# Gated linear attention: the two heads' half-height products issued in turn into two banks

## The chip, the cores and the metric

One core of one Trainium2 chip runs the whole program. The metric is the time of one execution on the device in microseconds (us); where several runs are compared, it is their median. The five engines of a core are TensorE (PE in the rows, its weight loads PEld), VectorE (DVE), ScalarE (ACT), GpSimd (POOL) and SyncE (SP).

## The reference

The program is one inference step of a two-layer decoder for 512 prompt tokens and 8 sample tokens at a model width of 1024. Layer 0 mixes tokens with differential attention and with gated linear attention (GLA), layer 1 with an mLSTM; each mixer stands between two half-step feed-forward blocks. The change touches only the GLA of the prompt: 4 heads with 64 key and 128 value features.

```python
b = jnp.cumsum(g, axis=2)                       # log decay, per key feature
decay = jnp.exp(jnp.where(causal, b_t - b_s, -inf))
a_intra = einsum('bnthd,bntshd,bnshd->bnhts', q, decay, k)
o_intra = einsum('bnhts,bnshv->bnthv', a_intra, v)
...
o_inter = einsum('bnthd,bnhdv->bnthv', q * exp(b), s_prev)
return o_intra + o_inter, s_fin
```

## The kernel before, in words

All tensors lie with features on the 128 partitions and tokens along the free dimension. Stage `even` is layer 0's mixer. Inside it `gla_pair(p, more)` runs twice, for p = 0 and p = 1. A pair is two heads: head i of the pair has its 64 key features on partitions 64i to 64i+63 of `bq[p]` and `bk[p]`.

A pair works on four chunks of 128 tokens (j = 0 to 3). Within a chunk the decay between two tokens is split by levels: at level lv the chunk falls into blocks of `64 >> lv` tokens, and the decay to the middle between two neighbouring blocks is folded into a scaled copy `gkq` of keys and queries (`level`, two DVE products per level). For each of the 8 masks (one for the diagonal, 7 levels) and each head, the inner function `masked` (lines 895 to 905) takes one PSUM bank, called `glv`, lets PE form four 128 by 128 products, one per chunk, with a contraction over the 64 partitions of that head (line 899), and lets DVE copy the masked entries into the head's matrix `A[i]` (`copy_predicated`, line 901). The products are in f32; the profile counts two PE records for each f32 product. Then `masked` calls `tick` and `aside`. At the end of a pair (lines 966 to 975), for each head in turn, a bank `go` collects per chunk `bv` times `A[i]` (contraction over 128, line 971) and, from the second chunk on, the state `S` times the scaled queries `qt` (contraction over the head's 64 partitions, line 974), and ACT evicts the bank to `ob`.

What else stands around these products on the in-order PE: `tick(us)` adds to an account, and whenever it holds more than 1.65 it issues a step of the sample tokens' attention (`sample_steps`). In this part a step is 8 products `so` of 128 by 32 columns (line 776, four column groups of the array), and needs one `vtile` of two pages (2 x 256 KB) that SP's queue loads from the cache; four such buffers rotate. `aside` advances generators that share the time: `gla_sample` (products `gsu` with a contraction over 8 partitions, line 1011, and `gso`), the head norms (`hs`, `hst`, `bc`) and splits. `decays` forms the decays of a level (`gdc`, line 914). `more` yields the projections of the output gate, `pj` (lines 100 to 102, full-height products); all four of its yields are used up in pair 0. After pair 1 stands the output projection, `y`, on the same three lines.

The banks for `glv`, `go`, `gdc`, `hs`, `bc` and the like come from one pool, `pmm`, of four PSUM banks that rotate (`bank`, line 615). Two banks are kept for dense products and two for the long sums of the sample attention. A scheduler places the instructions on each engine's queue; each engine then takes its own queue in order.

Of the kernel before, what the change touches and what calls it, by code (L numbers as in the profile page):

```python
# [15 lines left out]
P = 128  # L16
D = 1024
KT = 8
SEQ = 512
# [15 lines left out]
STEP, ORATE, GLAX = 1.65, 3.3, 1.7  # L35
# [20 lines left out]
class Net:  # L56
# [829 lines left out]
    def gla_pair(self, p, more):  # L886

        nc, gl = self.nc, self.gl
        bv = self.bv[p]
        q, k = self.bq[p], self.bk[p]  # L890
        A = [gl.tile([P, 512], F32, tag=f"A{i}", name="A") for i in range(2)]
        for a in A:
            nc.gpsimd.memset(a, 0.0)

        def masked(i, lhs, rhs, lv):
            r = slice(64 * i, 64 * i + 64)
            ps = self.bank("glv")
            for j in range(4):
                nc.tensor.matmul(ps[:, j * P:j * P + P], lhsT=lhs[r, j * P:j * P + P], rhs=rhs[r, j * P:j * P + P],  # L899
                                 start=True, stop=True)  # L900
            nc.vector.copy_predicated(A[i].rearrange("p (j t) -> p j t", j=4),
                                      self.gmask[:, lv, None, :].to_broadcast([P, 4, P]),
                                      ps.rearrange("p (j t) -> p j t", j=4))
            self.tick(0.9 * GLAX)
            self.aside()

        def decays(lv, n):

            e = gl.tile([P, 2, 4, P], F32, tag="ge", name="ge", bufs=2)[:, :n]
            for j in range(4):  # L910
                ps = self.bank("gdc")
                r = self.lvl[:, lv * P:(lv + n) * P]
                for i, s in enumerate((self.gh, self.gl_)):
                    nc.tensor.matmul(ps[:, :n * P], lhsT=s[:, j, p * P:p * P + P], rhs=r, start=(i == 0), stop=(i == 1))
                nc.scalar.activation(e[:, :, j, :], ps[:, :n * P].rearrange("p (l t) -> p l t", l=n), AF.Exp)
                self.tick(0.12 * n * GLAX)
            return e.rearrange("p l j t -> p l (j t)")

        if p == 0:
            next(more, None)  # L920
        ec = decays(7, 2)
        es = [decays(0, 2)]
        eb, er = ec[:, 0, :], ec[:, 1, :]
        qt = gl.tile([P, 512], F32, tag="gqt", name="gqt")
        nc.vector.tensor_tensor(out=qt, in0=q[:, :SEQ], in1=eb, op=ALU.mult)
        nc.vector.tensor_tensor(out=er, in0=k[:, :SEQ], in1=er, op=ALU.mult)
        next(more, None)
        kn = gl.tile([P, 4, P], F32, tag="gkn", name="gkn")
        self.natural(kn, None, er)
        S = []  # L930
        for j in range(4):
            ps = self.bank("gu")
            for i in range(2):
                nc.tensor.matmul(ps[64 * i:64 * i + 64, :P], lhsT=kn[:, j, 64 * i:64 * i + 64],
                                 rhs=bv[:, j, i, :], start=True, stop=True)
            s = gl.tile([P, P], F32, tag=f"S{j}", name="S")
            if j == 0:
                self.evict(s, ps[:, :P])
            else:
                nc.vector.scalar_tensor_tensor(s, S[-1], eb[:, j * P + P - 1:j * P + P], ps[:, :P], ALU.mult, ALU.add)  # L940
            S.append(s)
        nc.scalar.dma_start(out=self.t["o_gp"][p], in_=S[3])
        def level(lv):
            w = 64 >> lv
            ev = es[lv // 2][:, lv % 2, :].rearrange("p (n s w) -> p n s w", s=2, w=w)
            kv = k[:, :SEQ].rearrange("p (n s w) -> p n s w", s=2, w=w)
            qv = q[:, :SEQ].rearrange("p (n s w) -> p n s w", s=2, w=w)
            kq = gl.tile([P, 512], F32, tag="gkq", name="gkq", bufs=2)
            kqv = kq.rearrange("p (n s w) -> p n s w", s=2, w=w)
            nc.vector.tensor_tensor(out=kqv[:, :, 0, :], in0=kv[:, :, 0, :], in1=ev[:, :, 0, :], op=ALU.mult)  # L950
            nc.vector.tensor_tensor(out=kqv[:, :, 1, :], in0=qv[:, :, 1, :], in1=ev[:, :, 1, :], op=ALU.mult)
            return kq
        kq = level(0)
        for i in range(2):
            masked(i, k, q, 7)
        for lv in range(7):
            if lv in (0, 2):
                es.append(decays(lv + 2, 2))
            if lv == 4:
                es.append(decays(6, 1))  # L960
                next(more, None)
            now, kq = kq, level(lv + 1) if lv < 6 else None
            for i in range(2):
                masked(i, now, now, lv)
        next(more, None)
        for i in range(2):
            r = slice(64 * i, 64 * i + 64)
            o = self.bank("go")
            for j in range(4):
                oj = o[:, j * P:j * P + P]  # L970
                nc.tensor.matmul(oj, lhsT=bv[:, j, i, :], rhs=A[i][:, j * P:j * P + P],
                                 start=True, stop=(j == 0))
                if j:
                    nc.tensor.matmul(oj, lhsT=S[j - 1][r, :], rhs=qt[r, j * P:j * P + P], start=False, stop=True)
            self.evict(self.ob[:, 2 * p + i, :SEQ], o)

    def vtile(self):
        return self.ev.tile([P, T], F32, tag="vt", name="vt", bufs=2)
# [866 lines left out]
```

## Time and profile before

| | |
|---|---|
| median of three runs | 2262.44 us |
| the three runs | 2254.84, 2262.44, 2271.28 us |
| the profiled execution: its own time | 2272.11 us |
| the profiled execution: span from first to last instruction | 2270.3 us |
| mean granted TensorE clock over the span | 0.977 |
| busy over the span: PE, DVE, ACT | 2224.2, 1513.6, 1010.9 us |

A busy PE says only that products are in flight: they are pipelined, so how fast PE works is read from the distance between starts, not from the busy share. The granted clock (PEclk) is a share of full speed, 1.00 being 2.4 GHz and 0.50 being 1.2 GHz. In a row of the timeline the first number is the start, the second how long the merged group lasts, both in us; "x8" counts records, two for each f32 product.

### The profile page before, as it was taken

How to read it: one execution, taken by the hardware profiler on the slowest of the kernel's cores; microseconds unless marked ns; L12 is line 12 of the kernel's file. 1: busy time of each engine (PE TensorE's matmuls, PEld its weight loads, DVE VectorE, ACT ScalarE, POOL GpSimd, SP SyncE). 2: the span in 40 equal slices, each digit the busy share in tenths (PEclk: the TensorE clock that was granted, in tenths of full speed). 3: DMA queues.
4: the chain of work that ended last, by engine and by line, in shares of the span. 5: the costliest groups of instructions: out<-in, count | busy, mean ns of one | idle time of the engine just before them, and what ended most of it. 6: DMA issues, size and time to landing. Idle time of an engine off the chain costs nothing.

```text
span 2270.3 us, 45692 instructions
## 1 busy us (share of the span) xinstructions
PE 2224.2 (98%) x18340; PEld 2082.8 (92%) x18340; DVE 1513.6 (67%) x3161; ACT 1010.9 (45%) x1932; POOL 47.5 (2%) x112
## 2 busy tenths in 40 slices
PE   8999999999999999999999999999999999999999
PEld 8999998776776689999999999999889899999999
DVE  8858586435664478676768758586745588858683
ACT  6535354335522255344444535353545555525352
POOL 0000001000000000000000000000000000000000
PEclk9999999999996699999999999999999999999999
DMA  5324234587775552323223324232554464233322
GB/s 179 110 66 133 67 111 134 177 275 249 246 233 168 169 186 66 121 85 112 84 85 112 112 67 129 73 102 75 140 154 145 149 205 141 93 103 94 103 84 85
DMA packets 107019, 296.30 MB, mean 131 GB/s; under 512 B 12129, under 2 KB 16786, under 8 KB 106678
## 3 DMA queue, kind: packets, MB, share of 16 engines
q1 hardware_dynamic: 93504, 254.91, 35.3%
q0 software_dynamic: 7536, 25.42, 3.6%
q10 hardware_dynamic: 5766, 13.05, 1.6%
q8 instruction: 144, 2.36, 0.4%
q14 instruction: 69, 0.57, 0.1%
HBM read 276.22 MB, written 17.11 MB: 129 GB/s over the span
## 4 chain that ended last, share of the span: by engine, by line
PE 84%; DVE 6%; DMA 6%; ACT 2%; issue 2%; SPq 0%; POOL 0%; ACTq 0%; POOLq 0%; DVEq 0%
PE y L100 9%; PE y L101 8%; PE y L102 8%; PE A L100 6%; PE A L101 6%; PE A L102 6%; PE pj L100 3%; PE pj L101 3%; PE pj L102 3%; PE E L101 3%; PE E L100 3%; PE E L102 3%; DMA cs<-sc 2%; PE glv L899 2%; PE so L776 2%
## 5 line engine op out<-in xcount | busy, mean ns | idle before, releaser
L105 ACT CAST whi<-raw 128x512 fp32r<-128x512 f32 (+1 forms) x440 | 351.2, 806 | 435.0 <-PE y L101 171.3
L106 DVE TENSOR_TENSOR wlo<-raw,whi 128x512 fp32r<-128x512 f32 (+1 forms) x440 | 402.0, 922 | 156.4 <-ACT whi L105 142.5
L100 PE MATMUL y<-hh,whi 128*128 128x256 f32 (+1 forms) x1408 | 398.1, 283 | 0.0
L101 PE MATMUL y<-hl,whi 128*128 128x256 f32 (+1 forms) x1408 | 397.9, 283 | 0.0
L102 PE MATMUL y<-hh,wlo 128*128 128x256 f32 (+1 forms) x1408 | 396.8, 282 | 0.0
L100 PE MATMUL pj<-xh,whi 128*128 128x264 f32 (+1 forms) x896 | 263.8, 295 | 16.1 <-ACT gs L1531 3.2
L101 PEld LDWEIGHTS y<-hl,whi 128*128 128x128 f32 x1408 | 265.1, 188 | 1.0 <-DVE hl L106 0.6
L100 PEld LDWEIGHTS y<-hh,whi 128*128 128x128 f32 x1408 | 264.7, 188 | 0.8
L102 PEld LDWEIGHTS y<-hh,wlo 128*128 128x128 f32 x1408 | 264.8, 188 | 0.0
L102 PE MATMUL pj<-xh,wlo 128*128 128x264 f32 (+1 forms) x896 | 257.4, 288 | 2.9 <-DVE wlo L106 2.9
L101 PE MATMUL pj<-xl,whi 128*128 128x264 f32 (+1 forms) x896 | 258.6, 289 | 0.0
L100 PE MATMUL A<-xb,whi 128*128 128x264 f32 (+1 forms) x864 | 249.3, 290 | 0.7
L101 PE MATMUL A<-xb,whi 128*128 128x264 f32 (+1 forms) x864 | 244.2, 284 | 0.0
L102 PE MATMUL A<-xb,wlo 128*128 128x264 f32 (+1 forms) x864 | 243.0, 284 | 0.1
L105 ACT CAST whi<-graw 128x1024 fp32r<-128x1024 f32 x144 | 147.6, 1049 | 162.5 <-PE y L101 103.9
L100 PEld LDWEIGHTS pj<-xh,whi 128*128 128x128 f32 x896 | 173.1, 193 | 33.1 <-issue 10.3
L549 DVE SCALAR_TENSOR_TENSOR x<-y,x 128x256 f32<-128x256 f32 (+1 forms) x192 | 81.9, 427 | 180.5 <-PE y L102 180.1
L106 DVE TENSOR_TENSOR wlo<-graw,whi 128x1024 fp32r<-128x1024 f32 x144 | 172.6, 1219 | 30.9 <-ACT whi L105 30.9
L102 PEld LDWEIGHTS pj<-xh,wlo 128*128 128x128 f32 x896 | 172.9, 193 | 5.0 <-DVE wlo L106 3.3
L101 PEld LDWEIGHTS pj<-xl,whi 128*128 128x128 f32 x896 | 173.2, 193 | 4.0 <-issue 3.5
L100 PEld LDWEIGHTS A<-xb,whi 128*128 128x128 f32 x864 | 162.5, 188 | 9.2 <-DVE c L476 2.6
L100 PE MATMUL E<-xh,whi 128*128 128x264 f32 x576 | 163.7, 284 | 1.6 <-ACT whi L105 1.6
(468 smaller groups left out, 5179.9 us busy)
## 6 DMA issues: line engine op xcount, KB each, us to landing
raw<-w SPq DMA_DIRECT2D x240, 512.0 KB, 3.6
graw<-w SPq DMA_DIRECT2D x72, 512.0 KB, 4.4
kt<-ckt SPq DMA_DIRECT2D x128, 256.0 KB, 4.3
vtile<-cv SPq DMA_DIRECT2D x128, 256.0 KB, 3.7
raw<-w POOLq DMA_DIRECT2D x40, 512.0 KB, 4.5
cs<-sc SPq DMA_DIRECT2D x16, 512.0 KB, 6.9
kb<-kqd SPq DMA_DIRECT2D x16, 512.0 KB, 6.9
o_cs<-cs ACTq DMA_DIRECT2D x16, 512.0 KB, 5.3
```

The source lines that it names most:

```text
L100: nc.tensor.matmul(ps, lhsT=wh, rhs=xh, start=(ends[0] and i == ks[0]), stop=False, skip_group_check=open_)
L101: nc.tensor.matmul(ps, lhsT=wh, rhs=xl, start=False, stop=False, skip_group_check=open_)
L102: nc.tensor.matmul(ps, lhsT=wl, rhs=xh, start=False, stop=(ends[1] and i == ks[-1]), skip_group_check=open_)
L105: self.nc.scalar.copy(out=hi, in_=src)
L106: self.nc.vector.tensor_tensor(out=lo, in0=src, in1=hi, op=ALU.subtract)
L549: nc.vector.scalar_tensor_tensor(xs, y[:, :n], -0.5, xs, ALU.mult, ALU.add)
L776: nc.tensor.matmul(o[32 * h:32 * h + 32, :P], lhsT=pw[:, i, h, :], rhs=vt[:, i % KU, h * P:h * P + P], start=(b == 0 and g == 0 and i == 0 ...
L899: nc.tensor.matmul(ps[:, j * P:j * P + P], lhsT=lhs[r, j * P:j * P + P], rhs=rhs[r, j * P:j * P + P], start=True, stop=True)
```

## The change: what it does

`masked` now takes both heads at once: it takes two banks, issues the eight products with the chunk as the outer loop and the head as the inner one, so that products on partitions 0 to 63 and 64 to 127 stand in turn, each head writing its own bank, and then issues both DVE copies. The two calls of `tick` and `aside` of a pair of heads follow behind. The output products are written in the same way: per chunk both heads' products with `A`, then both heads' products with `S`, into two `go` banks. No product, copy or transfer is added or removed.

```diff
-        def masked(i, lhs, rhs, lv):
-            r = slice(64 * i, 64 * i + 64)
-            ps = self.bank("glv")
+        def masked(lhs, rhs, lv):
+
+            ps = [self.bank("glv") for _ in range(2)]
             for j in range(4):
-                nc.tensor.matmul(ps[:, j * P:j * P + P], lhsT=lhs[r, j * P:j * P + P], rhs=rhs[r, j * P:j * P + P],
-                                 start=True, stop=True)
-            nc.vector.copy_predicated(A[i].rearrange("p (j t) -> p j t", j=4),
-                                      self.gmask[:, lv, None, :].to_broadcast([P, 4, P]),
-                                      ps.rearrange("p (j t) -> p j t", j=4))
+                for i in range(2):
+                    r = slice(64 * i, 64 * i + 64)
+                    nc.tensor.matmul(ps[i][:, j * P:j * P + P], lhsT=lhs[r, j * P:j * P + P],
+                                     rhs=rhs[r, j * P:j * P + P], start=True, stop=True)
+            for i in range(2):
+                nc.vector.copy_predicated(A[i].rearrange("p (j t) -> p j t", j=4),
+                                          self.gmask[:, lv, None, :].to_broadcast([P, 4, P]),
+                                          ps[i].rearrange("p (j t) -> p j t", j=4))
+            self.tick(0.9 * GLAX)
+            self.aside()
             self.tick(0.9 * GLAX)
             self.aside()
...
-        for i in range(2):
-            masked(i, k, q, 7)
+        masked(k, q, 7)
...
-            for i in range(2):
-                masked(i, now, now, lv)
-        next(more, None)
+            masked(now, now, lv)
+        next(more, None)
+        o = [self.bank("go") for _ in range(2)]
+        for j in range(4):
+            c = slice(j * P, j * P + P)
+            for i in range(2):
+                nc.tensor.matmul(o[i][:, c], lhsT=bv[:, j, i, :], rhs=A[i][:, c], start=True, stop=(j == 0))
+            for i in range(2 * (j > 0)):
+                r = slice(64 * i, 64 * i + 64)
+                nc.tensor.matmul(o[i][:, c], lhsT=S[j - 1][r, :], rhs=qt[r, c], start=False, stop=True)
         for i in range(2):
-            r = slice(64 * i, 64 * i + 64)
-            o = self.bank("go")
-            for j in range(4):
-                oj = o[:, j * P:j * P + P]
-                nc.tensor.matmul(oj, lhsT=bv[:, j, i, :], rhs=A[i][:, j * P:j * P + P],
-                                 start=True, stop=(j == 0))
-                if j:
-                    nc.tensor.matmul(oj, lhsT=S[j - 1][r, :], rhs=qt[r, j * P:j * P + P], start=False, stop=True)
-            self.evict(self.ob[:, 2 * p + i, :SEQ], o)
+            self.evict(self.ob[:, 2 * p + i, :SEQ], o[i])
```

On PE, in the last levels of pair 0 (levels 4 and 5, of 0 to 6), the order before is this; the number behind a name is the tile's own, so `glv_9735` is head 0's bank and `glv_9790` head 1's.

```order
L776 MATMUL so_8348<-vtile_9721,pw_4509 32x128 x8
L899 MATMUL glv_9735<-gkq_9450 128x128 x4
L776 MATMUL so_8348<-vtile_9742,pw_4510 32x128 x8
L899 MATMUL glv_9790<-gkq_9450 128x128 x4
L776 MATMUL so_8348<-vtile_9796,pw_4510 32x128 x8
L899 MATMUL glv_9810<-gkq_9732 128x128 x4
L899 MATMUL glv_9816<-gkq_9732 128x128 x4
```

At the same place of the changed kernel stand, on PE, the first products of the same level, with `glv_9735` and `glv_9736` as the two heads' banks.

```order
L776 MATMUL so_8348<-vtile_9721,pw_4509 32x128 x8
L901 MATMUL glv_9735<-gkq_9450 128x128
L901 MATMUL glv_9736<-gkq_9450 128x128
L901 MATMUL glv_9735<-gkq_9450 128x128
L901 MATMUL glv_9736<-gkq_9450 128x128
```

The heads now alternate product by product, and the steps of the sample attention that stood between the two heads stand behind both.

For the output products of pair 0, PE has before, for the first of the two heads and the start of the second:

```order
L971 MATMUL go<-A,bv 128x128 x2
L974 MATMUL go<-gqt,S 128x128
L971 MATMUL go<-A,bv 128x128
L974 MATMUL go<-gqt,S 128x128
L971 MATMUL go<-A,bv 128x128
L974 MATMUL go<-gqt,S 128x128
L971 MATMUL go<-A,bv 128x128 x2
```

The changed kernel has on PE, for both heads together (the `x4` and `x2` alternate between the heads' banks):

```order
L973 MATMUL go<-A,bv 128x128 x4
L976 MATMUL go<-gqt,S 128x128 x2
L973 MATMUL go<-A,bv 128x128 x2
L976 MATMUL go<-gqt,S 128x128 x2
L973 MATMUL go<-A,bv 128x128 x2
L976 MATMUL go<-gqt,S 128x128 x2
```

The full-height products with `A` and the half-height ones with `S` change places 6 times in a pair, where they changed 12 times.

On DVE the same levels of pair 0 read before:

```order
L1173 RECIPROCAL br<-br 128x264
L901 COPY_PREDICATED A<-gmask,glv 128x512
L1174 TENSOR_TENSOR br<-br,pj 128x264
L901 COPY_PREDICATED A<-gmask,glv 128x512
L950 TENSOR_TENSOR gkq<-bk,ge 128x256
L951 TENSOR_TENSOR gkq<-bq,ge 128x256
L901 COPY_PREDICATED A<-gmask,glv 128x512 x2
```

And on DVE of the changed kernel:

```order
L1176 RECIPROCAL br<-br 128x264
L904 COPY_PREDICATED A<-gmask,glv 128x512
L1177 TENSOR_TENSOR br<-br,pj 128x264
L904 COPY_PREDICATED A<-gmask,glv 128x512
L955 TENSOR_TENSOR gkq<-bk,ge 128x256
L956 TENSOR_TENSOR gkq<-bq,ge 128x256
L771 COPY pw<-spt 128x16x2
L904 COPY_PREDICATED A<-gmask,glv 128x512 x4
```

The copies stand in the same order behind the same reciprocal; the banks that they free are now taken two at a time.

## Rows read from the trace of the kernel before

**Rows 1.** The page: busy engines over the span, and the granted clock in 40 slices.
```profile
PE 2224.2 (98%) x18340; PEld 2082.8 (92%) x18340; DVE 1513.6 (67%) x3161; ACT 1010.9 (45%) x1932; POOL 47.5 (2%) x112
...
PEclk9999999999996699999999999999999999999999
```
**Rows 2.** Stretches: PE, PEld, DVE, ACT, POOL busy (count), clock, DMA share, GB/s.
```profile
622.90:686.40 63.50, 63.32 (x708) 48.74 (x706) 44.14 (x115) 14.69 (x42) 2.95 (x11) 0.97 0.75 243
686.40:701.10 14.70, 14.70 (x179) 10.83 (x179) 7.49 (x20) 6.27 (x19) 0.52 (x3) 1.00 0.61 189
701.10:776.20 75.10, 75.10 (x448) 48.13 (x447) 25.21 (x75) 9.31 (x24) 1.85 (x6) 0.50 0.39 124
776.20:802.00 25.80, 25.24 (x281) 19.15 (x278) 16.05 (x52) 10.87 (x23) 2.28 (x5) 1.00 0.84 283
```
**Rows 3.** The chain that ended last, 615 to 805 us: three of its pieces.
```profile
668.81 4.09 DMA vtile<-cv
...
703.02 2.00 PE glv L899 x8
...
793.20 6.99 DMA vtile<-cv
```
**Rows 4.** Timeline of PE, pair 0, levels at full clock.
```profile
662.79 1.08 PE L776 MATMUL so<-vtile,pw 128*32 128x128 f32 x32
663.81 1.16 PE L899 MATMUL glv<-gkq 64*128 64x128 f32 x8
664.89 0.64 PE L776 MATMUL so<-vtile,pw 128*32 128x128 f32 x16
665.47 1.16 PE L899 MATMUL glv<-gkq 64*128 64x128 f32 x8
```
**Rows 5.** Timeline of PE: scores of the prompt attention, one half, then both halves.
```profile
511.32 0.48 PE L803 MATMUL aps<-kn,qn 64*128 64x128 f32 x2
511.74 0.44 PE L629 MATMUL tr<-ident,vt 128*128 128x128 f32 x2
...
546.39 0.49 PE L803 MATMUL aps<-kn,qn 64*128 64x128 f32 x4
546.81 0.39 PE L100 MATMUL pj<-xh,whi 128*128 128x256 f32 x1
```
**Rows 6.** Timeline of PE: output products, pair 0 and the end of pair 1.
```profile
680.98 0.71 PE L971 MATMUL go<-A,bv 128*128 128x128 f32 x4
681.62 0.48 PE L974 MATMUL go<-gqt,S 64*128 64x128 f32 x2
682.04 0.49 PE L971 MATMUL go<-A,bv 128*128 128x128 f32 x2
...
770.94 0.79 PE L971 MATMUL go<-A,bv 128*128 128x128 f32 x2
771.66 0.79 PE L974 MATMUL go<-gqt,S 64*128 64x128 f32 x2
```
**Rows 7.** Timeline of PE just before the clock falls at 701 us.
```profile
699.26 1.07 PE L1011 MATMUL gsu<-vt,ks 8*64 8x512 f32 x4
700.27 1.32 PE L899 MATMUL glv<-gkq 64*128 64x128 f32 x8
```
**Rows 8.** Waits (us in total, times, longest): 620:701, 701:777, PEld in 622:777.
```profile
DVE A L901 <- PE glv L899: 9.3, 11, 2.7
...
DVE A L901 <- PE glv L899: 16.7, 11, 3.2
...
PEld glv L899 <- DVE S L940: 0.4, 1, 0.4
```
**Rows 9.** Timeline of DVE in pair 0: what stands ahead of a masked copy.
```profile
664.37 1.80 DVE L1173 RECIPROCAL br<-br 128x264 f32<-128x264 f32 x1
```
**Rows 10.** Stretches of 5 us: DMA at its highest, and the dip in pair 0.
```profile
615.00:620.00 5.00, 5.00 (x54) 4.67 (x53) 4.90 (x12) 1.01 (x2) 0.00 (x0) 1.00 1.02 372
...
640.00:645.00 5.00, 5.00 (x34) 2.78 (x30) 3.03 (x15) 0.00 (x0) 0.00 (x0) 0.81 0.75 233
```

## The prediction

> **What bounds the kernel now.** I read the busy shares first: PE is in flight for 2224 of 2270 us, and the row of the granted clock has one dent, slices 13 and 14 [rows 1]. So PE sets the time, and there is a place where it runs slowly. I then cut the part that the change touches into stretches [rows 2]. Pair 0 takes 63.5 us at a clock of 0.97. Pair 1 takes 14.7 us at full clock and then 75.1 us at 0.50, half clock, although PE is in flight for all 75.10 of them. Both pairs together take 153.3 us. In none of these stretches is another engine full: DVE has 44.1 of 63.5 us in pair 0 and 25.2 of 75.1 in the slow one. DMA has a share of 0.75 in pair 0 and 0.39 in the slow part. The chain that ended last runs over PE, with two pieces of waiting for the cache pages, 4.09 and 6.99 us [rows 3]. The waits say the same from the other side: DVE waits for the products 22 times, 26 us together, while the products waited for DVE once, 0.4 us [rows 8].
>
> How fast PE goes within its busy time is read from starts. Four products of one head take 1.08 us from start to start (663.81 to 664.89), a step of `so` between them 0.58 us (664.89 to 665.47), two steps in one block 1.02 us [rows 4]. At half clock the same four products take 2.00 us [rows 3].
>
> **Term 1, the paired products at full clock.** Is a half-height product on partitions 64 to 127 free beside one on 0 to 63? The prompt's scores show it: one half alone took 0.42 us until the next block started (511.32 to 511.74), and both halves, in two banks, also took 0.42 us (546.39 to 546.81), with twice the records [rows 5]. So eight products in turn should take 1.09 us, where two blocks of four took 2.16: 1.08 us less per call, 8 calls in pair 0, 8.6 us. One of two ends is nothing, if the pairs do not run side by side; the other is this. I take this, since the row is for the same shapes and two banks. By the order, the two steps of `so` then mostly stand in one block: 1.02 instead of 2 x 0.58, 0.13 us less, 8 times, 1.0 us.
>
> **Term 2, the output products.** In pair 0 a lone product takes 0.42 us (681.62 to 682.04) and a block of two 0.64 (680.98 to 681.62) [rows 6], so a change between full and half height costs 0.20 and each product 0.22. Before, that is two blocks of two and ten lone ones: 5.5 us. After, one block of four (1.08), three pairs with `S` that cost as one each (3 x 0.42) and two blocks of two (2 x 0.64): 3.6 us. The gain is 1.9 us, or 1.2 if the halves with `S` do not overlap.
>
> Terms 1 and 2 make 11.5 us in pair 0. What could keep it: pair 0 already moves 243 GB/s for 63.5 us, 15.4 MB [rows 2]. In 52.0 us that needs 296 GB/s; behind the pairs 283 GB/s were held for 25.8 us, and a 5 us stretch reached 372 [rows 2, 10]. The levels without `pj` between them ask for two steps, 1.05 MB, in 1.09 + 1.02 us, which is above 372 GB/s, and already before a wait of 4.09 us stood on the chain there [rows 3]. The four buffers carry some of it. I take 6.5 us of the 11.5, and keep 0 and 11.5 as ends.
>
> **Term 3, pair 1, and the clock.** Two ends can be worked out. If the clock stays at half where it is, two of eight calls gain 1.08 us and six gain 2.00 us: 14.2 us; the output products take 0.72 us each (770.94 to 771.66 [rows 6]) and each further one in a block (2.00 - 0.72) / 3 = 0.43; by pair 1's order fourteen lone ones (10.1 us) become four blocks of two (4 x 1.15) and four of one or of a pair side by side (4 x 0.72), 7.5 us, which gains 2.6. Together that is 17 us, and pair 1 falls from 89.8 to 73. If the clock stays full throughout, the 75.1 us shrink by the ratio of equal blocks, 1.08/2.00 for the products and 0.42/0.72 for the output, about 0.56, to 42 us, which is 33 us less. On top stand the same terms as in pair 0, 8 x 1.08 + 1.9, about 10 us. Pair 1 falls to about 47 us, 43 less.
>
> Which end? Before the fall at 701 us PE did four products `gsu` that use 8 of 128 partitions, and half-height products [rows 7]. It stayed at half through levels made of half-height products of one head at a time, and rose only when the dense `y` products began at 776 us. Pair 0 has the same levels and the same `gsu`. There the clock dipped only around 640 to 645 us [rows 10], where `pj` products follow, and the mean is 0.97 [rows 2]. In the changed kernel both halves of the array work in the levels, so pair 1's levels come nearer to dense work, while the `gsu` products stay as they are. I expect short dips in place of one long stay: the clock comes back for most of pair 1, which takes 54 us, nearer to the full end. That is 36 us less.
>
> **Term 4, what comes late next.** Behind the pairs the wait of 6.99 us for pages [rows 3] and a DMA share of 0.84 over 25.8 us [rows 2] show that this part already runs at the transfers' pace. If pair 1 is shorter, less is loaded ahead: 2 us more here, between 0 and 7. The copies and the level products on DVE are the same ones, and DVE has 19 us of room in pair 0.
>
> **The sum.** The profiled execution took 2272.1 us. 2272.1 - 6.5 - 36 + 2 = 2231.6; rounded up for dips that I cannot place, 2234 us. That execution is the slowest of those shown: the median of the three runs is 9.7 us lower, and the runs spread over 16 us. If that spread is how long the clock stays low, the change takes most of it away, so I do not shift the sum.
>
> **The rivals.**
>
> *The clock stays at half through pair 1.* For it: it stayed there for 75 us of unbroken work [rows 2], and the changed order has `gsu` at the same place. Against it: twice the array at work in every level. Then 2272.1 - 6.5 - 17 = 2248.6 us, about 2248. The Trainium skill, TensorE: Matmul & The Clock Gate, section Why this matters for your kernels, says to keep the matmuls going without idle gaps to stay at the high clock; by that rule alone a PE without gaps is already at full clock, and a change that leaves PE as busy would move the clock nowhere. The trace does not agree: 0.50 with 75.10 of 75.10 us in flight [rows 2].
>
> *Transfers take over pair 0 and the part behind.* For it: the 4.09 and 6.99 us waits [rows 3]. Against it: at pair 0's own 243 GB/s all 27.5 MB of both pairs (15.4 + 2.8 + 9.3) need 113 us, 40 less than the 153.3 now. Term 1 and 2 gain nothing in pair 0 and the tail costs 5: 2272.1 - 36 + 5 = 2241 us.
>
> *Banks: the slower case.* A call now takes two of the four `pmm` banks, so two calls fill the pool, and the third waits until DVE has emptied a pair. A copy can stand behind a reciprocal of 1.80 us [rows 9]; with a copy of 0.7 us ahead, PE could wait 2.5 us in each of 16 calls, 40 us, and a waiting PE would leave the clock at half: 2272.1 + 40 - 11.5 - 17 = 2284 us. It decides from 28.5 / 16 = 1.8 us of waiting per call. Against it: DVE is there before the products in 22 of 32 copies [rows 8], and there are only two reciprocals among the last levels of pair 0. The Trainium skill, TensorEngine Tiling, section PSUM Bottleneck, warns that running tiles side by side speeds up TensorE but not the emptying of PSUM; no run here shows it yet.
>
> *The change does not do what it says:* the halves do not overlap in a stream of such pairs, since the scores show one pair at a time. Then only the fewer changes of height are left, some 5 us: 2267 us.
>
> **How the numbers follow.** The forecast, 2222 to 2246 us, gets 0.53; the clock at half 0.20; the transfers 0.15; the banks 0.07; no overlap 0.05. About 1% of 2262.4, 22.6 us, is what a measurement of this kernel can tell from no change, so faster means below 2239.8. Of the forecast 0.48 lies there, of the transfers' case half, 0.07, and of the half-clock case, where a run with a shorter low stretch may start 10 us lower, 0.08: 0.63. The banks are the slower case, 0.05 of their 0.07 by more than 1%. The rest, 0.32, is within. The low end has pair 0's whole 11.5 and pair 1's whole 43, 2217.6, and 4 us less for the spread of the runs: 2214. The high end takes in the half-clock case: 2252.
>
> **What would show it.** In the changed profile eight `glv` products (16 records) should take about 1.09 us from start to start at full clock; the step fails if they take 1.7 us or more. The clock over pair 1 should be above 0.85; at 0.60 or less the half-clock rival holds. Both pairs together should take about 111 us. PE waits named `glv` behind DVE copies of over 1 us would show the banks, and `so` waiting for pages by over 8 us in pair 0 the transfers. The forecast is wrong if the time is above 2252 us.

## The result, and the profile after

The changed kernel takes 2226.51 us (median of 4 runs, 2224.18 to 2230.07) where the kernel before, on the same chip, took 2258.64 (2254.77 to 2271.28). The ratio is 0.9876, with a 95% interval of 0.9829 to 0.9922. Six more runs, beside other runs of before, gave 2226.68 us and 0.9894 (0.9842 to 0.9945). The forecast was 2234 us with a range of 2214 to 2252, so time and sign came out as forecast. Ratios leave out disturbed runs of either kernel (those over 1.5% above its fastest), so with the long spread of before a ratio need not be the quotient of two medians.

The profiled execution after took 2225.22 us, 46.9 less than the profiled one before. Its page, the busy engines and the granted clock in 40 slices, answers to [rows 1]:

```profile
PE 2175.6 (98%) x18340; PEld 2052.0 (92%) x18340; DVE 1512.1 (68%) x3161; ACT 1009.9 (45%) x1932; POOL 47.4 (2%) x112
...
PEclk9999999999999999999999999999999999999999
```

The counts of instructions are the same, PE is in flight 48.6 us less, and the dent in the clock is gone. The same stretches as in [rows 2], in the changed kernel (start and end, length, then PE, PEld, DVE, ACT, POOL busy with counts, clock, DMA share, GB/s): pair 0, pair 1, the part behind, and the one dip in pair 1.

```profile
624.10:680.20 56.10, 53.47 (x705) 40.76 (x704) 42.87 (x113) 13.39 (x39) 2.32 (x10) 0.97 0.82 262
680.20:734.30 54.10, 53.68 (x639) 36.99 (x640) 31.68 (x94) 15.21 (x44) 2.99 (x10) 0.94 0.71 237
734.30:760.00 25.70, 22.82 (x267) 17.62 (x267) 16.91 (x55) 11.49 (x26) 2.27 (x5) 1.00 0.84 279
...
702.70:709.50 6.80, 6.80 (x64) 4.80 (x63) 3.15 (x10) 1.19 (x4) 0.00 (x0) 0.51 0.62 210
```

The pairs took 63.5 and 89.8 us before and take 56.1 and 54.1 now: 43.1 of the 46.9 us. The clock still falls in pair 1, but for 6.8 us, not 75.

PE's timeline shows the blocks themselves. First come two calls of `masked`, each with the row that follows it, then the output products of pair 0, then the only place in the pairs where PE's row has a product that waited for a masked copy. "x16" is eight products.

```profile
625.14 1.66 PE L901 MATMUL glv<-bq,bk 64*128 64x128 f32 x16
626.73 0.64 PE L214 MATMUL hs<-sq,one 128*32 128x256 f32 x8
...
630.31 1.16 PE L901 MATMUL glv<-gkq 64*128 64x128 f32 x16
631.41 0.64 PE L776 MATMUL so<-vtile,pw 128*32 128x128 f32 x16
...
676.91 1.16 PE L973 MATMUL go<-A,bv 128*128 128x128 f32 x8
678.00 0.49 PE L976 MATMUL go<-gqt,S 64*128 64x128 f32 x4
678.42 0.71 PE L973 MATMUL go<-A,bv 128*128 128x128 f32 x4
...
680.13 0.49 PE L976 MATMUL go<-gqt,S 64*128 64x128 f32 x4
680.55 0.39 PE L919 MATMUL gdc<-lvl,gh 128*128 128x256 f32 x1
...
729.26 0.71 PE L973 MATMUL go<-A,bv 128*128 128x128 f32 x4 [0.41 <-DVE A L904]
```

Eight products in turn take 1.10 us from start to start (630.31 to 631.41), as four of one head did [rows 4]. The pair of `S` products takes 0.42 us (678.00 to 678.42), as a lone one did [rows 6], and all output products of pair 0 take 3.64 us (676.91 to 680.55). The first call of a pair is the exception, 1.59 us in pair 0 (625.14 to 626.73) and 1.26 in pair 1: in pair 0 two products of one head start before the first of the other.

The waits from 624 to 765 us, both pairs and the part behind, answer to [rows 8] (in all, times, longest):

```profile
DVE A L904 <- PE glv L901: 13.6, 10, 2.8
...
PE so L776 <- DMA vtile<-cv: 4.4, 5, 2.2
```

DVE still waits for the products, half as long as before (13.6 against 26.0 us). No wait of a `glv` product for a bank is among the rows.

Where the rest of the 46.9 us lies is found by cutting both traces at the same instruction. Behind the pairs, from the sums over the sample tokens (`sf`) to a projection in layer 1, over the next stretch, and from there on; before first:

```profile
802.12:1641.64 839.52, 830.26 (x6750) 818.03 (x6748) 605.13 (x1108) 390.23 (x686) 7.11 (x16) 0.99 0.32 102
1641.64:1695.39 53.75, 48.32 (x350) 45.15 (x350) 28.33 (x81) 26.90 (x62) 1.11 (x3) 0.94 0.48 146
```

and the changed kernel:

```profile
760.35:1598.77 838.42, 830.29 (x6749) 818.06 (x6749) 606.66 (x1115) 392.29 (x690) 7.10 (x16) 0.99 0.32 102
1598.77:1647.17 48.40, 45.68 (x351) 42.59 (x351) 26.52 (x75) 24.56 (x57) 1.11 (x3) 1.00 0.50 159
```

The long stretch differs by 1.1 us. The short one is 5.35 us shorter with the clock up (1.00 against 0.94) in layer 1, which the change does not touch: I take that as the luck of one execution. Ahead of the pairs the changed kernel is 1.2 us later, and the rest makes up about +1.4 us. 1.2 - 43.1 - 1.1 - 5.35 + 1.4 gives the 46.9.

### The profile page after: what moved, and what is told of

Its sections match the earlier page's. It is cut to its first block, busy times and chain, and to the rows that moved or that the text cites. A ratio compares the mean times of both kernels' runs of the same rounds, so it can differ in the third digit from the quotient of the medians.

```text
span 2223.4 us, 45693 instructions
## 1 busy us (share of the span) xinstructions
PE 2175.6 (98%) x18340; PEld 2052.0 (92%) x18340; DVE 1512.1 (68%) x3161; ACT 1009.9 (45%) x1932; POOL 47.4 (2%) x112
## 4 chain that ended last, share of the span: by engine, by line
PE 84%; DVE 6%; DMA 6%; ACT 2%; issue 2%; POOL 0%; SPq 0%; ACTq 0%; POOLq 0%
PE y L100 9%; PE y L101 9%; PE y L102 9%; PE A L100 6%; PE A L101 6%; PE A L102 6%; PE pj L100 4%; PE pj L101 3%; PE pj L102 3%; PE E L101 3%; PE E L100 3%; PE E L102 3%; DMA cs<-sc 2%; PE sps L730 2%; PE u L102 1%
```

## The experiments

Twelve kernels ran in three groups, each beside its own runs of before; three of them are before (e0), the changed kernel (e10) and e1 (e11) once more. My theory was that the halves of the array work side by side, which shortens each block, and that this also keeps the clock from its long stay at half. Its rivals were that longer blocks alone do it, that dense work decides, or that the clock is no matter of the level products at all.

**Order alone or overlap: e1_grouped_serial, e9_grouped_kept_apart, e11_grouped_again.** In e1 both heads share a call as in the changed kernel, but the loops are swapped, and the output products stay as before:

```diff
-            for j in range(4):
-                for i in range(2):
+            for i in range(2):
+                for j in range(4):
```

> Both heads' products of a level stand in one block and the ticks behind them, as in the changed kernel, but all four of head 0 come first and then all four of head 1; the output products are as before. Theory (the gain needs the two halves of the array to work side by side): a block of 16 glv records takes about 2.0 us at full clock, the clock over pair 1 is near 0.5 to 0.6, and the time is 2250 to 2262 us, at most 5 us below before. Rival (the gain comes from the new grouping and order of the steps): about 2227 us.

Measured: 2232.34 us (2226.2 to 2234.62, 4 runs, clock 0.993 to 0.995), ratio 0.9871 (0.9818 to 0.9924). My own theory's number missed: this order was nearly as fast as the change. Its timeline says why:

```profile
632.63 1.71 PE L901 MATMUL glv<-gkq 64*128 64x128 f32 x16
634.27 0.65 PE L776 MATMUL so<-vtile,pw 128*32 128x128 f32 x16
```

The block takes 1.64 us, neither 1.09 nor twice 1.08: where products of one half directly follow those of the other, the second head starts while the first still runs. Before already showed this at the one place where its two heads were adjacent, in the first call of pair 1:

```profile
693.45 1.71 PE L899 MATMUL glv<-bq,bk 64*128 64x128 f32 x16
695.09 0.42 PE L776 MATMUL so<-vtile,pw 128*32 128x128 f32 x6
```

So e1 did not part grouping from overlap. e9 does: e1 with one small full-height product between the heads.

```diff
             for i in range(2):
+                if i:
+                    nc.tensor.matmul(ps[1][:, :1], lhsT=self.ident, rhs=self.ones, start=True, stop=True)
                 for j in range(4):
```

> As e1_grouped_serial (both heads' products of a level in one block, head 0's four and then head 1's four), with one full-height product of 128 by 1 column (the identity times a column of ones, into head 1's bank, which head 1's first product overwrites) between the two heads. A full-height product occupies both halves, so head 1 cannot start beside head 0. Theory A (the gain comes from the two halves working side by side, which e1 had in part: 16 records in 1.63 us): the block now takes 2.1 to 2.5 us from start to start at full clock, 0.5 to 0.9 us more in 16 blocks, 8 to 14 us, and the low clock of the kernel before comes back in some runs: mean clock 0.980 to 0.990, 2244 to 2258 us. Theory B (the gain comes from the longer blocks alone, in which fewer steps of so and half-height products change places): the block also takes 2.1 to 2.5 us, but the clock stays at 0.992 or above and the time is 2232 to 2242 us.

Measured: 2251.47 us (2236.34 to 2272.12, 12 runs, clock 0.980 to 0.995), ratio 0.9978 (0.9939 to 1.0018). No gain is left that can be told from noise. The block in e9's timeline:

```profile
632.89 1.16 PE L903 MATMUL glv<-gkq 64*128 64x128 f32 x8
633.98 0.38 PE L900 MATMUL glv<-ones,ident 128*128 128x1 f32 x2
634.29 1.16 PE L903 MATMUL glv<-gkq 64*128 64x128 f32 x8
635.37 0.64 PE L776 MATMUL so<-vtile,pw 128*32 128x128 f32 x16
```

It takes 2.48 us, of which 0.31 is the separator (16 times, 5 us). And a long stay at half clock is back. Pair 1 of e9 had 0.73 over 76.2 us, which is some 41 us at half; the second row is the stretch that holds most of it:

```profile
692.70:768.90 76.20, 76.20 (x632) 54.65 (x634) 33.06 (x92) 14.57 (x41) 2.31 (x9) 0.73 0.48 159
709.50:747.10 37.60, 37.60 (x246) 26.35 (x248) 12.58 (x38) 3.95 (x12) 0.25 (x2) 0.54 0.42 141
```

Theory A of e9 holds in its block, in the median of its times and in its median clock (0.9895). But its runs fall into two sets: six at a clock of 0.980 to 0.987, which took 2258 to 2272 us, and six at 0.992 or above, which took 2236 to 2244, as theory B had it. Of the 74 runs of before only 12 are at 0.992 or above. So without overlap the blocks gain nothing (below, at equal clock), but overlap is not shown to be all that keeps the clock: the grouping may hold it up in part. Nor is it shown whether the low clock came back because the overlap was gone or because of the separator itself, a product of one column put between them; no run tells these two apart.

What the changed kernel has over e1, alternating levels and alternating output products together, was measured on one chip, with the next run as its partner.

> e1_grouped_serial once more (head 0's four products, then head 1's four, in one block; output products as before). Theory: its block of 16 records takes 1.63 us against 1.09 us, 0.54 us more in 16 calls, 8.6 us, and its output products have 1.9 us more in each pair; the transfers keep a part of it. So it is 4 to 10 us slower than the changed kernel on this chip, 2228 to 2238 us. Rival: the grouping alone does it, and the two kernels are within 3 us of each other.

> The changed kernel once more, on the same chip as the next three. From its four runs so far (2224 to 2230 us at 0.991 to 0.993): 2222 to 2232 us, clock 0.989 to 0.995, with a half-clock stretch of under 15 us in the pairs where there is one.

Measured: e11 2235.49 us (2228.63 to 2240.63, 12 runs), e10 2226.68 us (2224.78 to 2233.36, 6 runs), both at a median clock of 0.992. The change is 8.8 us faster than grouping at the same clock, inside the 4 to 10 us; "within 3 us" falls. e10's profile has the clock at half for 7 us in each pair, under the 15 us expected.

**The parts: e2_alternate_levels_only, e3_alternate_output_only.** e2 is the changed kernel with the output products of before; e3 is before with the output products of the change.

> The changed kernel with the output products in before's order. Theory: the level products alone carry the clock and most of the time, 2228 to 2236 us, pair 1 at a clock above 0.85. Rival (the output products, a dozen changes of height at the end of each pair, matter as much): 2240 us or more.

> The kernel before with only the output products alternating. Theory: 1.9 us less in pair 0 and 2.6 us in pair 1 at half clock, so 2252 to 2258 us, and the clock stays low through pair 1. Rival: 2240 us or less.

Measured: e2 2232.59 us (2228.82 to 2241.39, 7 runs), ratio 0.9914 (0.9869 to 0.9959); e3 2254.59 us (2236.86 to 2267.98, 10 runs, clock 0.977 to 0.993), ratio 0.9994 (0.9954 to 1.0034). The levels carry most of the gain. The 6 us between e2 and the changed kernel come from separate groups; what the output products add is read below, at equal clock. One thing in e3 contradicts what I had written: its profiled execution kept full clock in pair 1, though its levels are those of before.

```profile
687.10:741.30 54.20, 54.16 (x603) 37.52 (x601) 31.76 (x92) 13.89 (x41) 2.60 (x10) 1.00 0.71 227
```

**Is the long stay a property of before, or a draw? e0_before_again.** The kernel before, unchanged.

> The kernel before once more, for a second profile. If the 75 us at half clock in pair 1 are one draw from a spread, this execution shows another length of it, and its time stands to its mean clock as in the runs so far, about 2.2 us per 0.001 (2242 at 0.992, 2260 at 0.982, 2272 at 0.977). If the fall after the gsu products belongs to the program, pair 1 is at 0.50 for 70 us or more again.

Measured: 2254.38 us at a clock of 0.986. Pair 1, and the low part in it:

```profile
689.00:762.30 73.30, 73.25 (x602) 49.46 (x601) 31.77 (x92) 14.56 (x41) 2.31 (x9) 0.72 0.50 163
709.50:747.60 38.10, 38.10 (x224) 25.25 (x225) 13.66 (x45) 5.25 (x15) 0.25 (x2) 0.51 0.44 146
```

0.72 over 73.3 us is 41 us at half (710.0 to 751.0; the second row ends before it does), where the first profile had 75. Its timeline at the fall:

```profile
706.60 1.16 PE L899 MATMUL glv<-gkq 64*128 64x128 f32 x8
707.69 0.43 PE L776 MATMUL so<-vtile,pw 128*32 128x128 f32 x8
708.04 1.07 PE L1011 MATMUL gsu<-vt,ks 8*64 8x512 f32 x2
709.04 0.43 PE L776 MATMUL so<-vtile,pw 128*32 128x128 f32 x8
709.39 1.44 PE L1011 MATMUL gsu<-vt,ks 8*64 8x512 f32 x2
710.77 0.58 PE L914 MATMUL gdc<-lvl,gh 128*128 128x256 f32 x1
```

Again it falls at a `gsu`, but at the second group of them, where the first profile fell just behind the first group [rows 7]. Over all 74 runs of before in the three groups, the time goes from 2232.91 to 2273.11 us and follows the mean clock: a straight line through them has 1.96 us per 0.001, with 2241.7 us at 0.992 and 2261.3 at 0.982, and the runs scatter by 1.9 us around it. So the length of the stay is a draw, and the clock goes with nearly all of the spread of before.

With this line each kernel can be compared at its own clock. The runs of e10 lie 13.2 us below it on average and the first four of the changed kernel 15.4, those of e2 8.6, of e1 6.4, of e11 5.6, of e3 3.0; single runs scatter by 2 to 3 us. At equal clock, then, grouped levels are worth about 6 us, alternating them about 3 more, and the output products 3 to 5 (e3; e10 against e2). e9 lies 5.4 us above the line, near the 5 us of its separators, and e8, which follows, within 0.1 us of it.

**What starts the stay: e8_no_gsu_in_pair1, e4_dense_into_pair1, e14_before_gsu_apart.** e8 leaves the `gsu` products of pair 1 out.

```diff
             ps = self.bank("gsu")
-            for i in range(2):
+            if p:
+                nc.vector.memset(ps, 0.0)
+            for i in range(2 * (1 - p)):
```

> The kernel before, without the eight-partition products gsu of pair 1 (their bank is filled with zeros by DVE instead, so the sample tokens' GLA states of heads 2 and 3 miss their update). The products themselves take about 1.07 us each two at full clock, 4 to 6 us together in pair 1. Theory A (the gsu products start the fall of the clock, as the rows before 701 us suggested): pair 1 stays at full clock, mean clock 0.990 or above, 2232 to 2242 us. Theory B (the half-height products of one head at a time, with little dense work between, are enough, and gsu is only a small part): the clock keeps its spread over the runs, 0.978 to 0.993, and the median is 2248 to 2256 us, lower than before by the 4 to 6 us of the products alone.

Measured: 2238.03 us (2233.42 to 2246.87, 12 runs, clock 0.990 to 0.995), ratio 0.9928 (0.9897 to 0.9959), as theory A said. The four products take 3 us at full clock (1.0 for the first two, 1.0 for each of the others), but at equal clock e8 is no faster than before: all of the 20 us go with the clock. Pair 1 of e8, whose levels are those of before:

```profile
688.10:741.30 53.20, 53.20 (x591) 37.88 (x594) 31.50 (x91) 14.32 (x41) 1.75 (x7) 1.00 0.65 213
```

e4 moves dense work near the levels instead: the fourth output gate projection goes from the end of pair 0 into pair 1. There it reads inputs that the side work has partly replaced, so its values are not the program's; the products are the same in number and shape.

```diff
-        next(more, None)
+        if p == 0:
+            next(more, None)
...
-        next(more, None)
```

> The kernel before with the fourth dense gate projection moved from the end of pair 0 into pair 1's levels; all products stay in before's form. Theory (the clock stays low in pair 1 because its work leaves most of the array idle, and comes back with denser work): the clock rises within or soon after the projection, pair 1 is at half clock for 20 to 50 us instead of 75, and the time is 2235 to 2252 us. Rival (only the alternating products move the clock): 2255 us or more and a clock of 0.5 through pair 1.

Measured: 2251.26 us (2243.3 to 2258.91, 10 runs, clock 0.984 to 0.990), ratio 0.9956 (0.9927 to 0.9985). Pair 0, pair 1 and the low part of its profile:

```profile
624.90:686.10 61.20, 59.85 (x611) 44.19 (x610) 37.38 (x105) 12.73 (x38) 2.54 (x9) 0.89 0.66 223
686.10:754.80 68.70, 68.69 (x711) 49.29 (x710) 37.54 (x102) 16.74 (x45) 2.76 (x10) 0.95 0.61 201
672.30:692.80 20.50, 20.42 (x125) 14.78 (x126) 3.94 (x9) 5.44 (x14) 1.30 (x4) 0.51 0.47 164
```

The low clock moved to the end of pair 0, where the projection now is missing, and no `gsu` stands there. So `gsu` is one start among others. Behind 692.6 us pair 1 kept full clock, and no run of e4 had a mean clock below 0.984, where 38 of the 74 of before did: dense work in pair 1 kept the longest stays away, much as its theory said, in this profile at the price of a stay elsewhere. What the starts have in common stays open. Here PE had stood still for a page as the clock fell at 672.1 us:

```profile
672.38 1.28 PE L776 MATMUL so<-vtile,pw 128*32 128x128 f32 x16 [1.35 <-DMA vtile<-cv]
```

The changed kernel's short dip in pair 0 (half clock from 665.1 us) also came behind a wait for a page, of 2.19 us, and one of e11's behind 1.71. And its dip in pair 1 came behind `gsu` and `gdc`, with alternating levels, so serial levels are not what all falls share.

e14 only spreads the `gsu` products of pair 1, and e13 does the same to the changed kernel:

```diff
                 nc.tensor.matmul(ps[64 * i:64 * i + 64, :], lhsT=ks[:, 64 * i:64 * i + 64],
                                  rhs=vd, start=True, stop=True)
+                if p and not i:
+                    yield
```

> The kernel before with the same edit: gsu products of pair 1 one at a time, everything else as before. If the lump of two sets off the long stay at half clock, it comes in fewer runs: 2236 to 2248 us, clock 0.988 or above. If what counts is that the gsu products are in pair 1 at all (without them it was 2238 us), spreading does not help: 2250 to 2260 us, clock 0.978 to 0.990.

> The changed kernel, with the two gsu products of a bank in pair 1 issued in two turns of the side work instead of one, so that in pair 1 they no longer stand next to each other; nothing else changes. If it is the lump of two eight-partition products that sets off the short fall in pair 1 (702.7 to 709.5 us in the changed kernel's profile), pair 1 keeps full clock in more runs: 2220 to 2228 us, clock 0.993 or above. Rival: the same products over a longer stretch only move the fall: within 4 us of the changed kernel.

Measured: e14 2252.68 us (2242.26 to 2270.9, 10 runs, clock 0.976 to 0.992), ratio 1.0015 (0.9973 to 1.0058); e13 2227.81 us (2221.03 to 2236.58, 10 runs, clock 0.989 to 0.996), ratio 0.9903 (0.9868 to 0.9939). Neither moved anything that can be told from its base; e14 went by its second case. That the two products stand next to each other is not shown to count.

**Is there more to get from the clock? e5_after_dense_in_pair1.** The changed kernel with the edit of e4.

> The changed kernel with the fourth projection of the output gate moved from the end of pair 0 into level 4 of pair 1 (its inputs are partly replaced by then, so this projection's values differ; shapes and counts are the same). If the clock still costs the changed kernel something in pair 1 (granted 0.94 there), dense work in it brings that back: clock 0.95 or above in pair 1, but a dip may come at the end of pair 0, where the projection is now missing; 2220 to 2230 us. If the alternating levels already keep the clock, the time stays within 4 us of the changed kernel's 2226.5, and a longer dip at the end of pair 0 would make it 2228 to 2236.

Measured: 2231.2 us (2223.26 to 2235.11, 6 runs, clock 0.987 to 0.993), ratio 0.9898 (0.9847 to 0.9948). In its profile pair 1 had a clock of 0.97, but its runs are no faster than the change's. Of the versions tried none beats the changed kernel by more than can be measured.

## Why the prediction was right, and where its reasons were not

*What bounds the kernel.* Right: the part works at PE's pace, and the gain lies where the pairs are.

*Term 1.* The step "eight products in turn should take 1.09 us" measured 1.09 to 1.10 at full clock. The count was off: the first call of each pair gained little, 2.17 to 1.59 us in pair 0 and 1.64 to 1.26 in pair 1, where before's heads already overlapped (693.45). The Trainium skill, TensorE: Matmul & The Clock Gate, section Part 3: Packing small matmuls — row/col tiling, says that products at different row positions run at the same time; this trace agrees, with 1.10 us for twice the work of 1.08. The prediction had drawn the same from the scores [rows 5].

*Term 2.* 3.6 us forecast for the output products of pair 0, 3.64 measured.

*What could keep it.* I took 6.5 of 11.5 us in pair 0; it was 7.4 (63.5 to 56.1). The transfers did keep a part: DMA went up to 262 GB/s in pair 0, and of the five waits of PE for pages, 4.4 us, two with 2.4 us lie in the pairs, the longest in pair 0.

*Term 3.* Pair 1 was to take 54 us and took 54.1; the clock was to lie above 0.85 and was 0.94; both pairs were to take 111 us and took 110.2. That 54 came out to 0.1 us is luck: it was a choice between 47 and 73, and e3's pair 1, with the levels of before at full clock, took 54.2 too. The reason, both halves at work, fits e1 and e9 together: in all 49 runs of the kernels with overlap (the changed one, e1, e2, e5, e10, e11, e13) the mean clock was 0.987 or above, where 58 of the 74 of before lay below, and without overlap, in e9, the low clock came back in six runs of 12. But one sentence before it failed as a description of the kernel: "It stayed at half through levels made of half-height products of one head at a time". That was one execution. Such levels ran at full clock in e3 and e8, and the stay was 41 us in e0. What the change does is to make the stay short, about 10 us at the longest in the seven profiles with overlap, not to end something that happened each time.

Two readings of rows were wrong. The "four products `gsu`" ahead of the fall are two, since "x4" counts records. And the clock did not rise as the dense `y` products began: some stood well inside the stay, at half clock.

```profile
749.30 0.58 PE L101 MATMUL y<-xl,whi 128*128 128x256 f32 x1
```

*Term 4.* "2 us more here" did not come. The stretch behind the pairs is as long as before within 0.1 us (25.7 against 25.8 [rows 2], at nearly the same transfer rate), and the 839.52 us after it became 838.42.

*The sum.* For the profiled execution it gave 40.5 us (2272.1 to 2231.6), and 46.9 came: the pairs gave 43.1 against 42.5, and the rest is the 2 us of term 4 that did not come and most of the 5.35 us of luck in layer 1. Not to shift it to the median was right for the reason given: the profiled execution before lay at the slow end of a spread which the change takes away. The 32 us between the medians (2258.6 to 2226.5) come in two parts. The line through the runs of before has 2241.7 us at a clock of 0.992, the changed kernel's; 2241.7 - 2226.7 = 15 us are the blocks, near the 6.5 us taken for pair 0 and the 10 us that term 3 gives the same products in pair 1. The other 17 us go with the clock, whose median went from 0.983 (all 74 runs of before) to 0.992 (9 x 1.96 is 17.6 us).

*The rivals.* The clock at half fell with pair 1 at 0.94. The transfers' case fell with the part behind. The banks fell: no `glv` product waited for a masked copy, and the only product that PE's rows put behind one waited 0.41 us, at 729.26 (in e10 and e13 `so` products waited 0.7 and 1.5 us in all). For the longest gap, 2.19 us up to 664.91, the weight loads' rows do name a masked copy, but the chain that ended last goes over the page. The Trainium skill, TensorEngine Tiling, section PSUM Bottleneck, warns that copying out of PSUM may become the limit when TensorE is sped up so; here it did not bind, since DVE was busy for 42.87 of 56.10 us in pair 0 and still waited for PE. No overlap fell with 1.10 us per call, and e9's block of 2.48 us shows what it would have been.

Not settled: what starts the stay, why it has a different length in each execution, and what ends it. No run tried to shift the moment of the fall while the instructions stayed the same.

## What to carry to other kernels

Two products of half height in the two halves of the array cost here as much as one when they stand next to each other in the order (1.10 us for eight, 1.08 for four), and one full-height product between the two heads' blocks, of a single column, took the overlap away (e9). So look for such pairs and write them in turn, with a bank each. Where a stretch of the profile shows half clock, take a second profile and set the runs' times against their mean clocks before you price it: part of the gain may be a draw that the other runs do not have. Making thin PE work denser can pay twice: here 15 us came in the blocks and 17 us with the clock.

## What the runs showed of the hardware that I had not expected

Serial order overlaps by itself in part: four products of one half and then four of the other took 1.64 us (632.63 to 634.27), not 2.16. That PE is in flight without a gap says nothing on its clock: the mean was 0.54 in e9 with 37.60 of 37.60 us in flight, and 1.00 in e8 with 53.20 of 53.20. And products that take 3 us at full clock, those of `gsu` in pair 1, were worth 20 us: without them the mean clock was 0.990 or above in all 12 runs, where 60 of the 74 of before lay below.
